# One channel tile as the running sum, and a new order of the first transfers, in a streaming-encoder layer

## The chip, the cores and the metric

The kernel runs on one core of one Trainium2 chip. The metric is the device time of one launch in microseconds (us). The kernel before took 2447.52 us as the median of three runs (2445.77 to 2451.0).

## What is computed

One layer of a streaming encoder, on 512 frames of 2048 channels, all in float32. Two mixers share one normalised input `h`: a gated DeltaNet attention (branch A) and a Conformer convolution module (branch B). The change touches branch B in one place, and the first load of the kernel in another.

```python
h = rmsnorm(x, g_pre[i])
proj = h @ w_in[i]
...
u = jax.nn.glu(glu_in, axis=-1)
u = causal_depthwise_conv(u, w_dw[i]) + b_dw[i]        # 31 taps, 2048 channels
u = jax.nn.silu(layernorm(u, ln_g[i], ln_b[i])) * jax.nn.silu(z_b)
y_b = u @ w_br_b[i]
...
e = p[i] @ w_ple_proj[i]
x = x + rmsnorm(jax.nn.sigmoid(x @ w_ple_gate[i]) * e, g_ple[i])
```

The layernorm needs the sum over all 2048 channels of each frame, so it needs the 16 tiles (128 channels by 512 frames each) of the filtered `u` added up.

## The kernel before, in words

Every float32 product is made of three float32r products: a weight tile is cast to a high part on ScalarE (ACT, L127), the low part is the difference (L128), and each pair of 128 by 128 weights and 128 by 512 activations takes three matmuls (L184, L186, L188: high by high, high by low, low by high). A raw weight load (L122, on SyncE's queue SP, three buffers) holds two pieces of 512 columns; a piece feeds 12 matmuls, and an output tile of the first projection (`gemm_cm`, L171) takes four pieces, 48 matmuls, into one of two PSUM buffers of the pool `gps`. The low part is made on VectorE (DVE) until the heads are done; then `low_part[0]` is set to GpSimd (POOL, L1058).

`load_x` (L226) is the opening. It splits the embedding rows `p` (`embed_in`, L197: two loads `pr`, a cast `ph`, a difference `pl`), loads the first weights of `w_ple_proj` through `prep` (L117), and multiplies the two (`embed`, L209, L216 to L218) while `x` arrives; the transposes that follow (L261) use the identity matrix, the first 128 columns of the tile `cst`, which L97 loads first of all.

Branch B's channels come as pairs of such 48-matmul groups (`glu_pair`, L991). The first group of a pair, for the gate, is taken out of PSUM by ACT (L911); the second by VectorE, which multiplies it with the gate (`evac_glu_a`, L978, the instruction at L981) into a tile `sg` and queues it for the filter. `convs` (L939) filters 14 of the 16 tiles on VectorE: a first scaling by ACT (L933), then 30 instructions of one line, L954, each of which adds a shifted and scaled `u` to the running result `y`. These are held in program order. `near` (L923) copies `u` into PSUM first (L930), if the pool `ups` exists; it does not yet exist for the very first tile, whose `u` is the `sg` tile in SBUF. In the profile the taps of that tile are `uc<-sg,vec,uc`, and those of the others `uc<-up,vec,uc`. `side_convs` (L964) filters two tiles with ACT (L972) and POOL (L973). A finished `y` is stored to DRAM (L961, on SP) for the layernorm to load again.

`filtered` (L915) keeps the channel sum `acc`. The first finished tile is copied into a tile of its own on POOL (L918); each later one is added to it on POOL (L920). `layer_norm` (L1134) multiplies the sum with ones on TensorE (L1143) and goes on from there.

Nothing in the code fixes the order of an engine's queue, save what is pinned: a list scheduler takes the program's instructions in order of priority as its own clock says that they are ready. Each engine and each DMA queue then works through its queue in order; an instruction that waits holds up all behind it.

Of the kernel before, what the change touches and what calls it, by code (L numbers as in the profile page):

```python
# [9 lines left out]
F32 = mybir.dt.float32  # L10
# [5 lines left out]
P = 128  # L16
T = 512
# [64 lines left out]
def _body(ctx, tc, A, out):  # L82
    nc = tc.nc
# [7 lines left out]
    slots = ctx.enter_context(tc.tile_pool(name="slots", bufs=21, side="right"))  # L91
# [2 lines left out]

    cst = const.tile([P, C_COLS], F32, name="cst")
    vec = const.tile([P, V_COLS], F32, name="vec")
    nc.sync.dma_start(cst[:, 0:P], A["consts"][:, 0:P])  # L97
    ident = cst[:, C_ID:C_ID + P]
    half_c = const.tile([P, 8], F32, name="half_c")
    nc.gpsimd.memset(half_c, 0.5)  # L100
# [8 lines left out]
    def vv(col, n=1):  # L109
        return vec[:, col:col + n]  # L110
# [6 lines left out]
    def prep():  # L117
        if not prep_src:
            return
        src = prep_src.popleft()  # L120
        raw = rawp.tile([P, 1024], F32, tag="raw", name="raw", bufs=3)
        nc.sync.dma_start(raw, src)  # L122
        for q in range(2):
            rq = raw[:, q * T:(q + 1) * T]
            w = ring.tile([P, 1024], F32R, tag="w", name="w")
            hi, lo = w[:, 0:T], w[:, T:]
            nc.scalar.copy(hi, rq)  # L127
            low_part[0].tensor_tensor(lo, rq, hi.bitcast(F32), ALU.subtract)  # L128
            hi_lo[id(hi)] = w.rearrange("p (s c) -> p s c", s=2)
            prepped.append((hi, lo))  # L130
# [66 lines left out]
    def embed_in():  # L197
        pT = []
        for k in range(2):
            pr = slots.tile([P, T], F32, tag="s", name="pr")  # L200
            nc.sync.dma_start(pr, A["pT"][k])
            ph = slots.tile([P, T], F32R, tag="s", name="ph")
            nc.scalar.copy(ph, pr)
            pl = slots.tile([P, T], F32R, tag="s", name="pl")
            nc.vector.tensor_tensor(pl, pr, ph.bitcast(F32), ALU.subtract)
            pT.append((ph, pl))
        return pT

    def embed(j, pT, xps):  # L209
        ps = [xps.tile([P, T], F32, tag="xp", name="e_ps") for _ in range(NTT)]  # L210
        for k in range(2):
            wh, wl = prepped.popleft()
            lh, ll = pT[k]
            for tt in range(NTT):
                b = slice(tt * P, (tt + 1) * P)
                mm(ps[tt], lh[:, b], wh, start=k == 0, stop=False)  # L216
                mm(ps[tt], lh[:, b], wl, start=False, stop=False)
                mm(ps[tt], ll[:, b], wh, start=False, stop=k == 1)  # L218
        for tt in range(NTT):
            e = slots.tile([P, T], F32, tag="s", name="e_sb")  # L220
            (nc.vector.tensor_copy if tt % 2 else nc.scalar.copy)(e, ps[tt])
            e_sb[j, tt] = e
# [3 lines left out]
    def load_x():  # L226
        with tc.tile_pool(name="xin", bufs=1) as xin, tc.tile_pool(name="xps", bufs=6, space=PSUM) as xps:
            xs = []
            H = D // 2
            prep_src.extend(A["w_ple_proj"][j] for j in range(4))  # L230
            prep_src.extend(first_src)
            pT = embed_in()
            prep()
            for tt in range(NTT):
                xt = xin.tile([P, D], F32, name=f"x{tt}")
                for hf in range(2):
                    nc.sync.dma_start(xt[:, hf * H:(hf + 1) * H], A["x"][tt * P:(tt + 1) * P, hf * H:(hf + 1) * H])
                if tt == 2:
                    nc.sync.dma_start(vec[:, 0:V_DW], A["vecs"][:, 0:V_DW])
                prep()  # L240
                embed(tt, pT, xps)
                ss = small.tile([P, 2], F32, tag="xss", name="xss")
                junk = xin.tile([P, H], F32, name="xjunk")
                for hf in range(2):
                    nc.scalar.activation(junk, xt[:, hf * H:(hf + 1) * H], AF.Square, accum_out=ss[:, hf:hf + 1])
                ms = small.tile([P, 1], F32, tag="xms", name="xms")
                nc.vector.tensor_tensor(ms, ss[:, 0:1], ss[:, 1:2], ALU.add)
                nc.vector.tensor_scalar(ms, ms, 1.0 / D, EPS, ALU.mult, ALU.add)
                rs = small.tile([P, 1], F32, tag="xrs", name="xrs")
                nc.gpsimd.tensor_tensor(rs, ms, mhalf_c[:, 0:1], ALU.pow)  # L250
                for hf in range(2):
                    nc.vector.tensor_scalar(xt[:, hf * H:(hf + 1) * H], xt[:, hf * H:(hf + 1) * H], rs, None, ALU.mult)
                xs.append(xt)
            nc.sync.dma_start(cst[:, P:], A["consts"][:, P:])
            nc.sync.dma_start(vec[:, V_DW:], A["vecs"][:, V_DW:])
            for (j, tt), e in e_sb.items():
                nc.sync.dma_start(pe_dram[j, tt], e)
            for k in range(NK):
                ps = xps.tile([P, T], F32, tag="xp", name="xp")
                for tt in range(NTT):  # L260
                    nc.tensor.transpose(ps[:, tt * P:(tt + 1) * P], xs[tt][:, k * P:(k + 1) * P], ident)  # L261
                hh = hpool.tile([P, T], F32R, tag="h", name="hh")
                hl = hpool.tile([P, T], F32R, tag="h", name="hl")
                nc.scalar.activation(hh, ps, AF.Copy, scale=vv(V_GPRE + k))
                nc.vector.scalar_tensor_tensor(hl, ps, vv(V_GPRE + k), hh.bitcast(F32), ALU.mult, ALU.subtract)
                hT.append((hh, hl))
# [11 lines left out]

    first_src = [w_in_tile(ZB_TILE0)[0], w_in_tile(ZB_TILE0)[1]]
    load_x()  # L280


# [617 lines left out]
    acc = []  # L900
# [13 lines left out]

    def filtered(i, y):  # L915
        if not acc:
            acc.append(slots.tile([P, T], F32, tag="s", name="acc"))
            nc.gpsimd.tensor_copy(acc[0], y)  # L918
        else:
            nc.gpsimd.tensor_tensor(acc[0], acc[0], y, ALU.add)  # L920
        done.add(i)
# [17 lines left out]
    def convs():  # L939
        ready = last = None  # L940
        while scanning[0] < NH // 2 - 1:
            yield 4
        while len(done) < NK:
            ready = ready or near()
            if not ready:
                if last and len(taken) == NK:
                    filtered(*last)
                    last = None
                yield 1
                continue  # L950
            (i, u, y), ready = ready, None
            w0 = V_DW + i * TAPS
            for s in range(1, TAPS):
                pin(nc.vector.scalar_tensor_tensor(y[:, s:], u[:, 0:T - s], vv(w0 + TAPS - 1 - s), y[:, s:], ALU.mult, ALU.add))  # L954
                if s == 28 and last:
                    filtered(*last)
                    last = None
                if s == 24:
                    ready = near()
                yield pace(s)  # L960
            nc.sync.dma_start(u_dram[i], y)  # L961
            last = i, y

    def side_convs():  # L964
        for _ in range(SIDE):
            while not waiting:
                yield 1
            i, u, y = near(False)
            w0 = V_DW + i * TAPS
            for s in range(1, TAPS):  # L970
                pr = s2.tile([P, T], F32, tag="s2", name="pr")
                nc.scalar.activation(pr[:, s:], u[:, 0:T - s], AF.Copy, scale=vv(w0 + TAPS - 1 - s))  # L972
                pin(nc.gpsimd.tensor_tensor(y[:, s:], y[:, s:], pr[:, s:], ALU.add))  # L973
                yield 18
            nc.sync.dma_start(u_dram[i], y)
            filtered(i, y)
# [643 lines left out]
    for tt in range(NTT):  # L1620
# [9 lines left out]
        for j in range(4):  # L1630
            s = e_t4[tt][j]
# [67 lines left out]
```

## Time and profile before

| | |
|---|---|
| median of three runs | 2447.52 us |
| the profiled execution's own time | 2447.55 us |
| its span, first instruction to last | 2445.8 us |
| TensorE (PE) busy | 2414.0 us, 99% |
| VectorE (DVE) busy | 1792.4 us, 73% |
| ScalarE (ACT) busy | 1208.8 us, 49% |
| GpSimd (POOL) busy | 507.0 us, 21% |
| DMA | 380.21 MB, mean 155 GB/s |

Times in rows of the profile count from the span's start. A row of the timeline is: start, length in us, engine, line, operation, output and inputs by the program's names, shapes, count, and in brackets how long the engine had been idle and what ended that. "SPq" and "ACTq" are the queues of SyncE and ScalarE, which issue DMAs. A matmul of 512 columns is listed at 0.39 us, but the next one starts 0.23 us after it, since they are pipelined. The column PEclk is the clock granted to TensorE as a share of full speed.

### The profile page before, as it was taken

How to read it: one execution, taken by the hardware profiler on the slowest of the kernel's cores; microseconds unless marked ns; L12 is line 12 of the kernel's file. 1: busy time of each engine (PE TensorE's matmuls, PEld its weight loads, DVE VectorE, ACT ScalarE, POOL GpSimd, SP SyncE). 2: the span in 40 equal slices, each digit the busy share in tenths (PEclk: the TensorE clock that was granted, in tenths of full speed). 3: DMA queues.
4: the chain of work that ended last, by engine and by line, in shares of the span. 5: the costliest groups of instructions: out<-in, count | busy, mean ns of one | idle time of the engine just before them, and what ended most of it. 6: DMA issues, size and time to landing. Idle time of an engine off the chain costs nothing.

```text
span 2445.8 us, 33732 instructions
## 1 busy us (share of the span) xinstructions
PE 2414.0 (99%) x11962; PEld 1985.5 (81%) x11962; DVE 1792.4 (73%) x3345; ACT 1208.8 (49%) x2357; POOL 507.0 (21%) x531
## 2 busy tenths in 40 slices
PE   8999999999999999999999998999999999999998
PEld 7888888887888888888888887888887888787886
DVE  7877888777677676867777678998998654667644
ACT  6455544554655656455555544454324533554532
POOL 0001110013213021132300005998740000000000
PEclk9999999999999999999999999999999999999999
DMA  7577776666536263556622222443534333665552
GB/s 270 162 199 199 202 201 208 207 162 204 175 119 185 87 185 93 171 168 178 181 90 90 67 91 79 138 137 104 170 118 166 131 122 99 232 216 173 188 173 77
DMA packets 145289, 380.21 MB, mean 155 GB/s; under 512 B 16352, under 2 KB 24800, under 8 KB 145120
## 3 DMA queue, kind: packets, MB, share of 16 engines
q1 hardware_dynamic: 119008, 319.32, 39.4%
q0 software_dynamic: 23808, 54.54, 10.3%
q10 hardware_dynamic: 2304, 4.20, 0.5%
q8 instruction: 94, 1.54, 0.3%
q14 instruction: 75, 0.61, 0.1%
HBM read 329.75 MB, written 48.23 MB: 155 GB/s over the span
## 4 chain that ended last, share of the span: by engine, by line
PE 89%; DVE 3%; POOL 2%; DMA 2%; issue 2%; ACT 2%; SPq 0%; POOLq 0%; DVEq 0%; ACTq 0%
PE g L186 13%; PE g L188 13%; PE g L184 13%; PE zp L423 6%; PE zp L421 6%; PE zp L422 5%; PE yp L1090 4%; PE yp L1094 4%; PE yp L1092 4%; PE f L1382 2%; PE f L1383 2%; PE f L1384 2%; PE f L1548 2%; PE f L1549 2%; PE f L1550 2%
## 5 line engine op out<-in xcount | busy, mean ns | idle before, releaser
L188 PE MATMUL g<-hh,w 128*128 128x512 f32 x1536 | 610.6, 397 | 4.1 <-POOL w L128 4.1
L186 PE MATMUL g<-hl,w 128*128 128x512 f32 x1536 | 611.3, 398 | 0.0
L184 PE MATMUL g<-hh,w 128*128 128x512 f32 x1536 | 609.5, 397 | 0.0
L127 ACT CAST w<-raw 128x512 fp32r<-128x512 f32 x588 | 357.9, 618 | 446.8 <-PE g L188 172.8
L128 DVE TENSOR_TENSOR w<-raw,w 128x512 fp32r<-128x512 f32 x464 | 321.5, 700 | 169.2 <-ACT w L127 166.6
L188 PEld LDWEIGHTS g<-hh,w 128*128 128x128 f32 x1536 | 289.8, 189 | 61.5 <-POOL w L128 5.4
L186 PEld LDWEIGHTS g<-hl,w 128*128 128x128 f32 x1536 | 289.6, 189 | 55.8 <-issue 1.4
L184 PEld LDWEIGHTS g<-hh,w 128*128 128x128 f32 x1536 | 289.9, 189 | 54.7 <-ACT w L127 0.9
L954 DVE SCALAR_TENSOR_TENSOR uc<-up,vec,uc 128x506 f32<-128x506 f32 (+29 forms) x390 | 284.0, 734 | 11.9
L128 POOL TENSOR_TENSOR w<-raw,w 128x512 fp32r<-128x512 f32 x124 | 161.4, 1314 | 136.7 <-DVE uc L954 74.5
L656 DVE SCALAR_TENSOR_TENSOR cv<-g,vec,cv 128x511 f32<-128x511 f32 x144 | 106.4, 739 | 27.2 <-ACT cv L654 26.6
L1090 PE MATMUL yp<-w,uh 128*128 128x512 f32 x256 | 100.2, 392 | 0.7 <-DVE gt L1102 0.7
L1094 PE MATMUL yp<-w,ul 128*128 128x512 f32 x256 | 100.1, 392 | 0.0
L1090 PE MATMUL yp<-w,oh 128*128 128x512 f32 x256 | 100.0, 393 | 0.0
L1092 PE MATMUL yp<-w,uh 128*128 128x512 f32 x256 | 100.0, 391 | 0.0
L1092 PE MATMUL yp<-w,oh 128*128 128x512 f32 x256 | 99.6, 389 | 0.0
L1094 PE MATMUL yp<-w,ol 128*128 128x512 f32 x256 | 99.1, 389 | 0.0
L842 DVE TENSOR_TENSOR prod<-UT,VT 128x2 f32<-128x2 f32 (+30 forms) x248 | 88.4, 356 | 6.5
L1006 POOL DMA_DIRECT2D wsum<-in_w_out x96 | 76.1, 847 | 71.2 <-DMA wsum<-in_w_out 32.9
L1326 POOL TENSOR_TENSOR rmsm<-totm,mhalf_c 128x2 f32<-128x2 f32 x2 | 2.4, 1198 | 378.3 <-DVE totm L1324 378.3
L973 POOL TENSOR_TENSOR uc<-uc,pr 128x511 f32<-128x511 f32 (+29 forms) x60 | 77.8, 1297 | 3.7 <-ACT pr L972 2.5
L1382 PE MATMUL f<-wsp,oph 128*128 128x512 f32 x192 | 75.6, 394 | 1.7 <-ACT wsp L1363 1.7
(386 smaller groups left out, 4952.5 us busy)
## 6 DMA issues: line engine op xcount, KB each, us to landing
raw<-in_w_in SPq DMA_DIRECT2D x194, 512.0 KB, 3.4
wsum<-in_w_out POOLq DMA_DIRECT2D x96, 256.0 KB, 5.4
raw<-in_w_ple_gate SPq DMA_DIRECT2D x40, 512.0 KB, 3.5
wo_sums<-wsum POOLq DMA_DIRECT2D x64, 256.0 KB, 4.1
raw<-in_w_br_a SPq DMA_DIRECT2D x32, 512.0 KB, 3.4
raw<-in_w_br_b SPq DMA_DIRECT2D x32, 512.0 KB, 3.3
raw<-in_w_ga SPq DMA_DIRECT2D x24, 512.0 KB, 4.7
raw<-in_w_gb SPq DMA_DIRECT2D x24, 512.0 KB, 4.5
```

The costliest lines, as they stand in the source:

```text
L127: nc.scalar.copy(hi, rq)
L128: low_part[0].tensor_tensor(lo, rq, hi.bitcast(F32), ALU.subtract)
L184: mm(ps, wh, rh, start=(k == 0), stop=False)
L186: mm(ps, wh, rl, start=False, stop=False)
L188: mm(ps, wl, rh, start=False, stop=(k == NK - 1))
L421: mm(ps[pr][t], lh, wh, start=q + n == 0, stop=False)
L423: mm(ps[pr][t], lh, wl, start=False, stop=q == 3 and n == 1)
L954: pin(nc.vector.scalar_tensor_tensor(y[:, s:], u[:, 0:T - s], vv(w0 + TAPS - 1 - s), y[:, s:], ALU.mult, ALU.add))
L1090: mm(ps[tt], lh[:, b], wh, start=k == 0, stop=False)
L1092: mm(ps[tt], lh[:, b], wl, start=False, stop=False)
L1094: mm(ps[tt], ll[:, b], wh, start=False, stop=k == NK - 1)
L1382: mm(ps, lh, wh[:, c], start=kk == 0, stop=False)
```

## The change

Three edits. The tile of the first finished channel block becomes the sum itself, in place of a copy of it; the two loads of embedding rows are issued by ScalarE's queue, no longer by SyncE's; and the load of the identity matrix is written behind the first weight load. The identity matrix still comes before the loads of `x`.

```diff
     cst = const.tile([P, C_COLS], F32, name="cst")
     vec = const.tile([P, V_COLS], F32, name="vec")
-    nc.sync.dma_start(cst[:, 0:P], A["consts"][:, 0:P])
     ident = cst[:, C_ID:C_ID + P]
...
             pr = slots.tile([P, T], F32, tag="s", name="pr")
-            nc.sync.dma_start(pr, A["pT"][k])
+            nc.scalar.dma_start(pr, A["pT"][k])
             ph = slots.tile([P, T], F32R, tag="s", name="ph")
...
             pT = embed_in()
             prep()
+            nc.sync.dma_start(cst[:, 0:P], A["consts"][:, 0:P])
             for tt in range(NTT):
...
     def filtered(i, y):
         if not acc:
-            acc.append(slots.tile([P, T], F32, tag="s", name="acc"))
-            nc.gpsimd.tensor_copy(acc[0], y)
+            acc.append(y)
         else:
             nc.gpsimd.tensor_tensor(acc[0], acc[0], y, ALU.add)
```

## The prediction

> **What bounds the kernel now.** I read the page first, then TensorE's waits, then the timeline around the two longest of them.
>
> ```profile
> span 2445.8 us, 33732 instructions
> PE 2414.0 (99%) x11962; PEld 1985.5 (81%) x11962; DVE 1792.4 (73%) x3345; ACT 1208.8 (49%) x2357; POOL 507.0 (21%) x531
> PE e_ps L216 <- ACT w L127: 6.7, 1, 6.7
> PE g L188 <- POOL w L128: 4.1, 2, 3.5
> 1522.00:1527.00 5.00, 5.00 (x14) 3.88 (x13) 4.75 (x8) 1.04 (x3) 5.00 (x5) 0.51 0.68 218
> ```
>
> TensorE is the bound: it is idle for 2445.8 - 2414.0 = 31.8 us in all. Only what moves a TensorE wait can move the time. The opening (6.7 us) is the largest wait, and a wait of 3.5 us for a low part made on POOL is the second; in the stretch after it the granted clock (third figure from the row's end, 0.51) is half. The edits touch just these two places. Both are costed in the profiled execution (2447.55 us, of which the span is 2445.8), which stands 0.03 us from the median of 2447.52. About 0.2%, 4.9 us, is what a measurement of this kernel can tell from no change.
>
> **The wait at 1517, as it is.**
>
> ```profile
> 1509.06 0.39 PE L184 MATMUL g<-hh,w 128*128 128x512 f32 x1
> 1517.45 0.39 PE L186 MATMUL g<-hl,w 128*128 128x512 f32 x1
> 1521.29 0.79 PE L188 MATMUL g<-hh,w 128*128 128x512 f32 x1 [3.45 <-POOL w L128]
> 1525.72 0.63 PE L184 MATMUL g<-hh,w 128*128 128x512 f32 x1
> 1527.20 0.39 PE L186 MATMUL g<-hl,w 128*128 128x512 f32 x1
> 1510.25 1.72 POOL L128 TENSOR_TENSOR w<-raw,w 128x512 fp32r<-128x512 f32 x1
> 1519.40 0.61 POOL L918 COPY acc<-uc 128x512 f32<-128x512 f32 x1 [7.43 <-DVE uc L954]
> 1519.97 1.27 POOL L128 TENSOR_TENSOR w<-raw,w 128x512 fp32r<-128x512 f32 x1
> ```
>
> From 1509.06 to 1517.45 are 37 matmuls, 8.39 / 37 = 0.2268 us each. The next should start at 1517.68; it starts at 1521.29, 3.61 late. The following 14 steps to 1527.20 take 5.91 instead of 14 x 0.227 = 3.18: the half clock costs 2.73 more. Together 6.34 us. The cause is POOL's queue: the copy L918, which waits 7.43 us for the last tap of the first filter, stands ahead of the low part that TensorE needs.
>
> **The sum's copy removed.** POOL goes on at 1511.97 rather than 1519.40, and the low part is there at 1513.7, four microseconds before TensorE asks. If that were all, 6.3 us would be gone. It is not all, because VectorE is in the middle of that first filter.
>
> ```profile
> 1497.40 1.65 DVE L954 SCALAR_TENSOR_TENSOR uc<-sg,vec,uc 128x499 f32<-128x499 f32 x1
> 1510.86 1.64 DVE L954 SCALAR_TENSOR_TENSOR uc<-sg,vec,uc 128x491 f32<-128x491 f32 x1
> 1512.53 0.73 DVE L954 SCALAR_TENSOR_TENSOR uc<-sg,vec,uc 128x490 f32<-128x490 f32 x1
> 1519.26 0.74 DVE L954 SCALAR_TENSOR_TENSOR uc<-up,vec,uc 128x511 f32<-128x511 f32 x1
> 1519.92 0.68 DVE L981 TENSOR_TENSOR sg<-g,sg 128x512 f32<-128x512 f32 x1
> 1495.00:1511.00 16.00, 16.00 (x72) 13.26 (x71) 15.65 (x11) 9.24 (x16) 15.82 (x10) 1.00 0.21 67
> 1521.00:1540.00 19.00, 18.71 (x71) 15.25 (x72) 18.15 (x26) 7.83 (x13) 18.92 (x16) 0.84 0.51 164
> ```
>
> While POOL is busy (15.82 of 16 us from 1495 to 1511) a tap of this filter takes 1.65 us, and a POOL instruction 1.72; from 1497.40 to 1510.86 are eight taps, 13.46 / 8 = 1.68 from start to start. When POOL falls silent the same tap takes 0.73. The later filters, whose `u` lies in PSUM (`up`), do not suffer: from 1521 to 1540 POOL is busy for 18.92 of 19 us and taps still take 0.74. So the wait of POOL is also a free road for VectorE: the nine taps from 1512.53 to 1519.26 (6.73 / 9 = 0.75 from start to start) ran fast only because the copy held POOL. Does POOL have nine instructions' worth of ready work to put in their place?
>
> ```profile
> 1522.43 2.53 POOL L128 TENSOR_TENSOR w<-raw,w 128x512 fp32r<-128x512 f32 x2
> 1528.61 1.32 POOL L1069 TENSOR_TENSOR ol<-oa,oh 128x512 fp32r<-128x512 f32 x1
> 1529.86 2.58 POOL L128 TENSOR_TENSOR w<-raw,w 128x512 fp32r<-128x512 f32 x2
> 1501.79 2.55 ACT L972 ACTIVATE pr<-sg,vec 128x507 f32<-128x507 f32 x4
> 1515.29 1.14 ACT L1067 CAST oh<-oa 128x512 fp32r<-128x512 f32 x2
> 1517.47 0.62 ACT L127 CAST w<-raw 128x512 fp32r<-128x512 f32 x1 [1.04 <-issue]
> 1525.96 0.60 ACT L911 ACTIVATE sg<-g 128x512 f32<-128x512 f32 x1 [7.88 <-PE g L188]
> ```
>
> Behind the copy POOL runs, from 1519.97 to about 1531, without a gap: a low part, a side tap (L973), two low parts, a side tap, a head's low part (L1069), a side tap, another L1069, a low part. That is nine (11.2 us at about 1.25 each), and their inputs come from ACT: side products by 1504.3, casts of the heads by 1516.4, the last weight cast by 1518.1, all before POOL would reach them at one per 1.68 us. So all nine taps stay slow: the first ends its turn not at 1513.3 but at 1514.2, and the ninth at 1512.53 + 9 x 1.68 = 1527.65. Behind them in VectorE's queue stand one tap of the next filter and then L981, which now end 1519.92 + 0.68 - 1519.26 = 1.34 after the ninth tap; that gives 1528.99.
>
> Who waits for L981? It empties one of two PSUM buffers. The group that fills it began its successor at 1509.06 in the other buffer; that successor is 48 matmuls long and so would end at 1509.06 + 48 x 0.2268 = 1519.94 without a stall. In the trace its end is 1525.72, and ACT's L911 empties it at 1525.96. The next group must have L981's buffer. Today it is free at 1520.60, five microseconds early. After the change TensorE would stand from 1519.94 to 1529.04 (0.05 for the hand-over, as from POOL's 1521.24 to 1521.29): 9.10 us, and then run at half clock again.
>
> The price of that clock phase: 2.73 us at 1521, and in the opening
>
> ```profile
> 6.68 0.80 PE L216 MATMUL e_ps<-w,ph 128*128 128x512 f32 x1 [6.68 <-ACT w L127]
> 11.87 0.39 PE L216 MATMUL e_ps<-w,ph 128*128 128x512 f32 x1
> 13.36 0.50 PE L218 MATMUL e_ps<-w,pl 128*128 128x512 f32 x1 [0.64 <-DVE pl L205]
> ```
>
> 12 steps take 5.19 instead of 2.72, a loss of 2.47. I take 2.6. [...] So the place costs 9.1 + 2.6 = 11.7 after, 6.3 before: **+5.4 us**. Bounds: 2.2 to 3.2 for the clock and one tap (1.0) either way for the overlap give +4 to +7.
>
> What else moves there: the copy's own 0.61 us on POOL lies under TensorE's work. SP's store of the tile (L961) waits for the ninth tap too, and raw loads stand behind it; but the three raw buffers hold the pieces of the whole next group, which is on the wrong side of the stall. The next add L920 on POOL must wait for the second filter:
>
> ```profile
> 1543.30 0.59 ACT L930 COPY up<-sg 128x512 f32<-128x512 f32 x1 [2.53 <-DVE uc L954]
> 1545.08 1.30 POOL L920 TENSOR_TENSOR acc<-acc,uc 128x512 f32<-128x512 f32 x1
> 1546.34 1.30 POOL L128 TENSOR_TENSOR w<-raw,w 128x512 fp32r<-128x512 f32 x1
> 1551.24 0.39 PE L188 MATMUL g<-hh,w 128*128 128x512 f32 x1
>   PE g L188: 9.4, 7
> ```
>
> That filter ends with L930's release at 1543.3, and 8.4 later after the change, so the add comes at 1551.7, 6.6 later, with a low part behind it that TensorE uses 3.6 us after it is made (1547.64 to 1551.24). TensorE itself is 5.4 later: 1.2 of the 3.6 is eaten, nothing waits. VectorE then catches up: from 1520 to 1760 it sat idle before L981 seven times, 9.4 us (last row), waiting for TensorE, which is more than the 3 us that it is further behind.
>
> **The opening.**
>
> ```profile
> 0.74 0.38 SPq L97 DMA_DIRECT2D cst<-in_consts  x1
> 1.17 0.42 SPq L201 DMA_DIRECT2D pr<-in_pT  x1
> 1.64 0.42 SPq L122 DMA_DIRECT2D raw<-in_w_ple_proj  x1
> 6.01 1.14 ACT L127 CAST w<-raw 128x512 fp32r<-128x512 f32 x2 [1.49 <-DMA raw<-in_w_ple_proj]
> 12.62 0.68 DVE L205 TENSOR_TENSOR pl<-pr,ph 128x512 fp32r<-128x512 f32 x1
> ```
>
> TensorE starts 0.67 after that cast, which starts when `raw` lands. The issue of `raw` moves from 1.64 to 0.74, 0.9 us. ACT takes two issues (0.4 each) before data that it must wait for anyway. The same bytes are in flight, so the gain at 6.68 lies between 0 and the 0.9, or a little over since the small identity packets no longer go first. The 0.64 us before 13.36 is a wait for the second embedding row's low part, which VectorE makes at 12.62 behind work on `x`; if the row's earlier load brings it forward, that wait goes as well, and if not, it swallows what was won at 6.68. Between 0 and -2 I take **-1.2 us**. The identity matrix, one issue later, is first needed by the transposes behind all this, so it costs nothing; were it late, its 0.38 us issue is the price.
>
> Sum: 2447.55 + 5.4 - 1.2 = **2451.7 us**, 0.17% more: no change that a measurement would show, from a gain and a loss.
>
> **Rivals.** *The stall simply goes.* If the scheduler puts L981 ahead of the slow taps, or POOL's and VectorE's instructions overlap better than ten rows at 1.68 say, the buffer is free in time: 2447.55 - 6.3 - 1.2 = 2440.0. For it: the low part does come in time, and the order of VectorE's queue is the scheduler's, which no row shows for the changed program. Against it: L981 stands behind those taps today.
>
> *The engines exclude each other wholly.* Then a pair costs the two lengths alone, 1.27 + 0.73 = 2.00 instead of 1.68; nine pairs take 18.0, not 15.1, and L981 and TensorE come 2.9 us later: 2454.6, slower. It decides from a pair spacing of about 1.76 up, where nine pairs add the 0.7 us that are missing to 4.9. Ten rows in a row at 1.68 speak against it. [...]
>
> *The change does not free POOL.* If another instruction that waits for that filter takes the copy's place in POOL's queue, the stall stays: 2447.55 - 1.2 = 2446.3. The first add is the only candidate, and it needs the second filter as well, at 1545.08, so this is unlikely.
>
> **How the numbers follow.** My forecast's case has 0.58; of it 0.11 lies above 4.9 us (no gain in the opening gives 2447.55 + 5.4 = 2452.9). The vanishing stall has 0.25, the full lock 0.09, the stall that stays 0.08. Faster: 0.25. Same: 0.47 + 0.08 = 0.55. Slower: 0.11 + 0.09 = 0.20. The range must reach into the first rival to hold 8 in 10: 2439.0 to 2454.0; the forecast's own is 2449.5 to 2454.
>
> **What would show it.** Right: no L918; POOL without a gap after about 1510; nine more taps at 1.65; L981 about 8 us later; a TensorE wait of some 9 us on DVE L981 at the start of a group, then half clock; a first matmul near 5.8. Wrong: no TensorE wait at that place (first rival), a pair spacing near 2.0 (second), or POOL still waiting for DVE L954 (third).

## The result, and the profile after

The change made the kernel slower: 2455.32 us (median of seven runs, 2453.04 to 2458.22) against 2446.80 (seven runs of the kernel before beside it, 2445.04 to 2451.0). The ratio is 1.0033, with a 95% interval of 1.0022 to 1.0045: 8 us, with 5 to 11 us possible. The forecast was 2451.7 with a range up to 2454.0. The profiled execution took 2456.29 us. In the kernel after, most lines have moved up by one (the filter's taps are L953, the evacuation on VectorE is L980).

The page and TensorE's waits of the kernel after (in the waits: microseconds in total, how often, the longest):

```profile
span 2454.2 us, 33730 instructions
PE 2415.4 (98%) x11962; PEld 1986.8 (81%) x11962; DVE 1799.3 (73%) x3345; ACT 1209.2 (49%) x2357; POOL 510.6 (21%) x530
PE g L183 <- DVE sg L980: 9.8, 1, 9.8
PE e_ps L215 <- ACT w L126: 6.3, 1, 6.3
PE e_ps L215 <- ACT ph L202: 1.1, 1, 1.1
```

TensorE's longest wait is a new one. The wait for POOL at 1517 is gone from the list; in its place TensorE stands 9.8 us for the instruction by which VectorE empties a PSUM buffer. The timeline of the kernel after at that place:

```profile
1495.16 34.37 DVE L953 SCALAR_TENSOR_TENSOR uc<-sg,vec,uc 128x502 f32<-128x502 f32 x21
1515.76 3.40 POOL L127 TENSOR_TENSOR w<-raw,w 128x512 fp32r<-128x512 f32 x2
1519.13 1.70 POOL L972 TENSOR_TENSOR uc<-uc,pr 128x505 f32<-128x505 f32 x1
1520.79 1.69 POOL L1068 TENSOR_TENSOR ol<-oa,oh 128x512 fp32r<-128x512 f32 x1
1522.44 1.67 POOL L972 TENSOR_TENSOR uc<-uc,pr 128x504 f32<-128x504 f32 x1
1524.07 3.32 POOL L127 TENSOR_TENSOR w<-raw,w 128x512 fp32r<-128x512 f32 x2
1527.35 1.66 POOL L972 TENSOR_TENSOR uc<-uc,pr 128x503 f32<-128x503 f32 x1
1529.45 0.74 DVE L953 SCALAR_TENSOR_TENSOR uc<-up,vec,uc 128x511 f32<-128x511 f32 x1
1530.11 0.67 DVE L980 TENSOR_TENSOR sg<-g,sg 128x512 f32<-128x512 f32 x1
1520.70 0.39 PE L187 MATMUL g<-hh,w 128*128 128x512 f32 x1
1530.93 0.77 PE L183 MATMUL g<-hh,w 128*128 128x512 f32 x1 [9.84 <-DVE sg L980]
1537.04 0.40 PE L187 MATMUL g<-hh,w 128*128 128x512 f32 x1
```

The same 21 taps in the kernel before:

```profile
1494.17 25.17 DVE L954 SCALAR_TENSOR_TENSOR uc<-sg,vec,uc 128x502 f32<-128x502 f32 x21
```

Read the POOL rows first: each starts where the one before ends, so POOL no longer waits for the filter. The price stands in the first row: the 21 taps with both inputs in SBUF take 34.37 us, 9.20 more than before. From POOL's 1515.76 to 1527.35 are seven instructions, 11.59 / 7 = 1.66 us each, where the prediction had 1.68. Behind the last of the 21 taps come one tap of the next filter and then L980, which starts at 1530.11 and ends at 1530.78. TensorE, whose next matmul was due at 1520.70 + 0.23 = 1520.93, goes on at 1530.93. The 14 steps from there to 1537.04 take 6.11 us instead of 3.18, at half clock (granted 0.50). So the place costs 10.00 + 2.93 = 12.9 us, against 6.34 before: 6.6 more.

Set each matmul beside the same one of the profile before: the first of the kernel comes 0.4 us earlier, the one at 23.6 us 0.3 later, those near 1000 us at the same time, those from 1100 to 1480 1.1 later, those behind the stall 7.6 later, the last 8.4 later.

The opening of the kernel after:

```profile
0.74 0.38 SPq L121 DMA_DIRECT2D raw<-in_w_ple_proj  x1
0.74 0.40 ACTq L200 DMA_DIRECT2D pr<-in_pT  x1
5.08 0.62 ACT L202 CAST ph<-pr 128x512 fp32r<-128x512 f32 x1 [2.62 <-DMA pr<-in_pT]
5.08 0.35 ACTq L200 DMA_DIRECT2D pr<-in_pT  x1
5.60 1.13 ACT L126 CAST w<-raw 128x512 fp32r<-128x512 f32 x2
6.26 0.79 PE L215 MATMUL e_ps<-w,ph 128*128 128x512 f32 x1 [6.26 <-ACT w L126]
12.28 0.62 ACT L202 CAST ph<-pr 128x512 fp32r<-128x512 f32 x1 [2.83 <-DMA pr<-in_pT]
12.95 0.50 PE L215 MATMUL e_ps<-w,ph 128*128 128x512 f32 x1 [1.14 <-ACT ph L202]
```

The two first loads now leave together at 0.74, and the embedding rows land at 5.08 (before: 3.90). The weights' cast waits for no load any more: it stands behind the rows' cast on ScalarE, so it starts at 5.60 and TensorE at 6.26 rather than 6.68. The second load of rows is issued at 5.08, when ScalarE reaches it behind that first cast; before, SyncE issued it at 3.06. It lands late, its cast comes at 12.28, and TensorE waits 1.14 us for it.

### The profile page after: what moved, and what is told of

The parts are those of the page before. It is cut to its first block, busy times and chain, and to the rows that moved or that the text cites. A ratio compares the mean times of both kernels' runs of the same rounds, so it can differ in the third digit from the quotient of the medians.

```text
span 2454.2 us, 33730 instructions
## 1 busy us (share of the span) xinstructions
PE 2415.4 (98%) x11962; PEld 1986.8 (81%) x11962; DVE 1799.3 (73%) x3345; ACT 1209.2 (49%) x2357; POOL 510.6 (21%) x530
## 3 DMA queue, kind: packets, MB, share of 16 engines
q0 software_dynamic: 23808, 54.54, 10.2%
## 4 chain that ended last, share of the span: by engine, by line
PE 88%; DVE 5%; DMA 2%; POOL 2%; ACT 2%; issue 1%; SPq 0%; POOLq 0%; DVEq 0%; ACTq 0%
PE g L185 13%; PE g L187 13%; PE g L183 13%; PE zp L423 6%; PE zp L422 6%; PE zp L421 6%; PE yp L1089 4%; PE yp L1091 4%; PE yp L1093 4%; PE f L1381 2%; PE f L1382 2%; PE f L1383 2%; PE f L1549 2%; PE f L1548 2%; PE f L1547 2%; DVE uc L953 2%
## 5 line engine op out<-in xcount | busy, mean ns | idle before, releaser
L183 PEld LDWEIGHTS g<-hh,w 128*128 128x128 f32 x1536 | 290.3, 189 | 65.8 <-issue 10.2
L953 DVE SCALAR_TENSOR_TENSOR uc<-up,vec,uc 128x506 f32<-128x506 f32 (+29 forms) x390 | 283.9, 733 | 11.9
```

Of the source, the lines that this page charges most:

```text
L183: mm(ps, wh, rh, start=(k == 0), stop=False)
```

## The experiments

The theory is that of the prediction, made into a chain: POOL works on; it collides with the first filter's taps, because that filter alone reads its input from SBUF (before the change, beside a busy POOL: 1.65 us a tap, against 0.74 with the input in PSUM); the filter ends late; whatever waits for its end or stands behind it on VectorE is late, a PSUM buffer first of all. Against it stand two others: that the edits of the opening cost the time, or that the first tile, now held as the sum, does. In the list, times are medians, ratios are against runs of the kernel before on the same chip, with 95% intervals. The kernel before took 2445.58 us beside the first four kernels, 2446.01 beside the next four, 2446.03 beside the last four.

| run | median us | ratio | interval |
|---|---|---|---|
| the sum alone | 2451.79 | 1.0026 | 1.0015 to 1.0037 |
| the opening alone | 2447.61 | 1.0007 | 0.9999 to 1.0016 |
| the change, with POOL's wait, without the copy | 2446.48 | 1.0005 | 0.9996 to 1.0014 |
| the change, more PSUM buffers | 2453.16 | 1.0035 | 1.0022 to 1.0047 |
| the sum, first filter later | 2442.58 | 0.9987 | 0.9978 to 0.9996 |
| the sum, first filter's input to PSUM | 2439.69 | 0.9976 | 0.9966 to 0.9985 |
| the copy kept, first filter's input to PSUM | 2439.38 | 0.9972 | 0.9962 to 0.9983 |
| the sum, input to PSUM, opening in another order | 2438.77 | 0.9971 | 0.9961 to 0.9982 |
| rows on ScalarE's queue alone | 2447.47 | 1.0008 | 0.9999 to 1.0017 |
| identity matrix later alone | 2445.79 | 1.0000 | 0.9991 to 1.0009 |
| opening in another order alone | 2445.63 | 1.0002 | 0.9993 to 1.0011 |
| the change, input to PSUM | 2440.42 | 0.9979 | 0.9970 to 0.9988 |

**The sum alone, on the kernel before.**

```diff
-            acc.append(slots.tile([P, T], F32, tag="s", name="acc"))
-            nc.gpsimd.tensor_copy(acc[0], y)
+            acc.append(y)
```

> The kernel before with the edit of the sum alone; the opening is left as it was. Collision theory (with no copy to wait for, POOL works on beside the first filter, whose taps have both inputs in SBUF and so take 1.65 rather than 0.73 us; the evacuation that frees TensorE's PSUM buffer comes late): the whole loss is here, 2453 to 2456 us, with a TensorE wait of 9 to 10 us for the DVE instruction on sg near 1520, 21 taps in 34 us and some 13 us at half clock after it. Opening theory (the moved loads cost the time, the sum does not): 2446 to 2448 us, no change. The two stalls of about half a microsecond in the heads stage (1077 and 1089), which the changed kernel has and the kernel before has not: if they come from the opening, they are absent here and the time is nearer 2454; if from the sum, they cannot be, since they stand ahead of it.

Slower by 6.2 us (3.7 to 9.1 by the interval). Its timeline and its waits have the chain of the kernel after:

```profile
1493.14 33.23 DVE L953 SCALAR_TENSOR_TENSOR uc<-sg,vec,uc 128x502 f32<-128x502 f32 x21
PE g L184 <- DVE sg L980: 8.7, 1, 8.7
```

Most of the loss is the sum's. It is less than the 2453 to 2456 us expected: the wait is 8.7 us, not 9 to 10, and the half clock behind it lasted 10.2 us, not 13. Its matmuls lie 1.0 us ahead of those of before at 1510 and 4.0 behind at 1626: 5.0 us for the place in this execution.

**The opening alone: the changed kernel with the copy put back.**

```diff
-            acc.append(y)
+            acc.append(slots.tile([P, T], F32, tag="s", name="acc"))
+            nc.gpsimd.tensor_copy(acc[0], y)
```

> The changed kernel with the copy into a tile of its own put back: the opening edits alone. Collision theory: 2446 to 2449 us, within 0.2% of the kernel before; POOL waits 7 us for the last tap again, TensorE waits 3.5 us for a low part made on POOL near 1517, and no wait of 9 us. The opening itself gives its first wait back (6.3 against 6.7 us, then 1.1 against 0.6 us at the second half). Opening theory: 2453 to 2456 us. If the two half-microsecond stalls near 1077 and 1089 are seen here as well, they come from the opening edits and cost about 1 us: 2448.

Slower by 2.0 us, with -0.2 to +3.9 by the interval: no loss is shown, but a gain of 1.2 is outside it. The matmuls of its profile lie 0.3 us behind those of before at 23.6 us, and the last ones level with them. The waits of before are back (3.5 us for POOL's low part), that of 9 us is not there. The opening theory falls for the large part.

**POOL's wait without the copy.**

```diff
             acc.append(y)
+            seen = small.tile([P, 1], F32, tag="seen", name="seen")
+            nc.gpsimd.tensor_copy(seen, y[:, T - 1:T])
```

> The changed kernel, in which POOL copies one column of the first finished channel into a tile of its own (nothing reads it), so that POOL waits for the last tap as before, but the copy of 512 columns is left out and the finished tile still serves as the sum. Collision theory: the wait, not the copy, was what mattered; POOL idles about 7 us, 21 taps take about 25 us again, TensorE's wait is 3 to 3.5 us for the low part and not 9.8 us for VectorE, and the time is 2446 to 2449 us. Theory that the tile kept as the sum costs the time (its place in the pool of tiles is held longer, the first addition waits for it): 2455 us as in the changed kernel, with the wait of 9 to 10 us still there or another in its place.

```profile
1518.69 0.19 POOL L919 COPY seen<-uc 128x1 f32<-128x1 f32 x1 [7.44 <-DVE uc L955]
1493.45 25.18 DVE L955 SCALAR_TENSOR_TENSOR uc<-sg,vec,uc 128x502 f32<-128x502 f32 x21
PE g L187 <- POOL w L127: 3.7, 2, 3.0
```

0.9 us over the kernel before and, by the two ratios (1.0005 and 1.0033), 7 us under the changed one, although it has the same sum and the same opening. An instruction of 0.19 us that does nothing but wait 7.44 us makes the kernel faster by that much: while POOL stands, VectorE has the road for itself and ends its 21 taps in 25.18 us, not 34.37. The tile that serves as the sum costs nothing by itself.

**More PSUM buffers, in the changed kernel.**

```diff
-            ps = gps.tile([P, T], F32, tag="g", name="g")
+            ps = yps.tile([P, T], F32, tag="y", name="g") if early else gps.tile([P, T], F32, tag="g", name="g")
...
-        gemm_cm(w_in_tile(GLU_TILE0 + i), hT, evac_glu_a(i))
+        gemm_cm(w_in_tile(GLU_TILE0 + i), hT, evac_glu_a(i), 5 <= i < 10)
```

> The changed kernel with five groups of gated matmuls (numbers 5 to 9, those that stand around the first filter) put into another set of PSUM buffers, so that TensorE does not wait for the evacuation at the end of the filter. Collision theory in two steps, collision first and then the buffer: the taps stay at 1.65 us (POOL still works beside them), but the wait of 9.8 us for the DVE instruction and the half clock behind it go, and the time falls by 12 to 16 us to 2440 to 2444 us. If the buffer is not the link (TensorE would wait for something else that VectorE owes it just as late, or the other set is itself not free), the time stays at 2452 to 2456 us and the wait only changes its name.

The miss: 12 to 16 us were expected of it and it brought nothing that shows. The wait for L980 is gone, and two others stand in its place. The timeline (SyncE's queue, ScalarE, TensorE):

```profile
1527.03 0.33 SPq L960 DMA_DIRECT2D u_dram<-uc  x1
1527.45 0.38 SPq L121 DMA_DIRECT2D raw<-in_w_in  x1
1532.02 0.62 ACT L126 CAST w<-raw 128x512 fp32r<-128x512 f32 x1 [9.37 <-DMA raw<-in_w_in]
1532.69 0.62 PE L183 MATMUL g<-hh,w 128*128 128x512 f32 x1 [2.19 <-ACT w L126]
1550.95 0.59 ACT L929 COPY up<-sg 128x512 f32<-128x512 f32 x1 [12.59 <-DVE uc L953]
1552.14 0.51 PE L183 MATMUL g<-hh,w 128*128 128x512 f32 x1 [3.10 <-ACT w L126]
```

The store of the finished channel (L960) waits on SyncE's queue for the last tap, and the next weights are issued only behind it, at 1527.45; they land at 1532.02 and TensorE waits 2.19 us. Later ScalarE stands 12.59 us before the copy L929, which waits for VectorE, with weight casts behind it, and TensorE waits 3.10 us more. The PSUM buffer was the first of three links to the late filter; with it gone, the next two are met. So the middle of the chain, not its last link, has to be mended.

**The first filter later, with its input in PSUM.** The sum as in the change, without the copy, and the opening as before.

```diff
-        while scanning[0] < NH // 2 - 1:
+        while scanning[0] < NH // 2 - 1 or not ups:
             yield 4
```

> The kernel before with the edit of the sum, and the first filter does not begin until the PSUM pool for the filters' input exists, so that its input, like that of all the others, is copied into PSUM; POOL works on beside it as in the changed kernel. Collision theory: the taps take 0.74 us although POOL is busy all the time, the first filter ends no later than before (30 taps by 0.67 to 0.77 us from some 1497: 1517 to 1520), neither the wait of 3.6 us for POOL nor that of 9 us for VectorE is left, and the time is 2438 to 2443 us. If POOL's work slows VectorE whatever the place of its input, the taps stay at 1.65 us, the filter ends near 1545 and the time is 2455 us or more. If holding the tile as the sum were a cost of its own, 2450 us or more with taps at 0.74 us.

3.4 us under the kernel before, and no wait from 1500 to 1780 is left. Its taps (`uc<-up,vec,uc`) go at 14.70 us for 19, 0.77 each. It is 2.9 us slower than the next kernel. Its matmuls, set beside those of before, lose 4.0 us between 1760 and 2035, those of the next kernel nothing; TensorE waits there for VectorE's `gt` (1.10 us) and for a low part made there (1.09 us). Why was not pursued.

**The first filter's input moved to PSUM as soon as the pool exists.**

```diff
             for s in range(1, TAPS):
+                if ups and not held:
+                    held = True
+                    up = ups.tile([P, T], F32, tag="u", name="up")
+                    nc.scalar.copy(up, u)
+                    u = up
```

> The kernel before with the edit of the sum; the first filter begins as early as before, and as soon as the PSUM pool exists, its input is copied there by ScalarE (one copy of 0.6 us) and the taps left read it from PSUM. Collision theory: the 20 taps left take 0.67 to 0.77 us instead of 1.65 us, the first filter ends 5 us earlier than before (about 1514), no wait at 1517 to 1530 is left, and the time falls by the whole 6.3 us of the stall and its half clock: 2438 to 2441 us. If VectorE's lateness was not what TensorE waited for, 2450 to 2455 us as with the edit of the sum alone.

The timeline, and one row of the stretches (us, busy time and count of TensorE, its weight loads, VectorE, ScalarE, POOL; then the granted clock); the last row is the same stretch of the kernel after:

```profile
1492.79 14.52 DVE L959 SCALAR_TENSOR_TENSOR uc<-up,vec,uc 128x502 f32<-128x502 f32 x19
1507.98 0.69 DVE L986 TENSOR_TENSOR sg<-g,sg 128x512 f32<-128x512 f32 x1 [0.67 <-PE g L188]
1504.82 1.30 POOL L978 TENSOR_TENSOR uc<-uc,pr 128x507 f32<-128x507 f32 x1
1511.00:1527.00 16.00, 16.00 (x73) 13.23 (x72) 15.26 (x21) 8.53 (x16) 13.53 (x12) 1.00 0.44 147
```

```profile
1511.00:1527.00 16.00, 10.09 (x45) 8.03 (x43) 15.65 (x11) 5.37 (x9) 16.00 (x10) 0.89 0.05 20
```

TensorE is busy without a gap (73 matmuls instead of 45), at full clock (1.00 granted, against 0.89); VectorE does 21 instructions in the time of 11, and POOL's own fall from 1.7 to 1.3 us. VectorE even waits for TensorE before the evacuation, 0.67 us. The time is 6.3 us under the kernel before, as much as the whole stall of 1517 cost, and 12.1 us under the same kernel with the input left in SBUF, by medians. One copy of 0.6 us on ScalarE does it. The collision is the cause.

**The same, but with the copy kept.**

```diff
             acc.append(slots.tile([P, T], F32, tag="s", name="acc"))
             nc.gpsimd.tensor_copy(acc[0], y)
```

> The kernel before, with its copy of the first channel on POOL, and only the input of the first filter moved into PSUM as in the run before this one. Collision theory: the copy waits for a filter that now ends near 1513, while TensorE needs POOL's low part only at 1517.7, so the wait behind the copy becomes short enough to be hidden: 2438 to 2442 us, within 0.1% of the same kernel without the copy. The edit of the sum is then worth nothing, neither gain nor loss. If the copy cost TensorE something by itself, the stall of 3.5 us stays and the time is 2445 to 2448 us.

```profile
1510.87 0.61 POOL L918 COPY acc<-uc 128x512 f32<-128x512 f32 x1
```

The copy stands in the same place of POOL's queue and waits for nothing, because the filter has ended. 2439.38 against 2439.69: without the collision, the edit of the sum is worth nothing that can be measured, either way.

**The opening in another order.**

```diff
+        prs = [slots.tile([P, T], F32, tag="s", name="pr") for _ in range(2)]
         for k in range(2):
-            pr = slots.tile([P, T], F32, tag="s", name="pr")
-            nc.scalar.dma_start(pr, A["pT"][k])
+            nc.scalar.dma_start(prs[k], A["pT"][k])
+        for k in range(2):
+            pr = prs[k]
             ph = slots.tile([P, T], F32R, tag="s", name="ph")
```

> The edit of the sum and the first filter's input in PSUM, with the changed opening in another order: both loads of embedding rows are issued on ScalarE's queue ahead of the first cast, so that the second does not stand behind a cast that waits for the first. If the opening of the change lost its gain by that order alone, the first matmul starts at 5.8 to 6.4 us, the second half's wait of 1.1 us falls to 0.6 us or less, and the time is 0.5 to 1.5 us under the same kernel with the old opening, which a comparison can hardly tell; the profile can. If the loads are bound by something else (they share the DMA engines with the first weights and x), the second half still waits 1 us or more and the time is the same within 0.5 us.

> The kernel before with the whole opening of the change, but both row loads issued on ScalarE's queue ahead of the first cast; the sum is left as it was, with its copy and its stall. Queue-order theory: the second half's wait of 1.1 us is gone and the kernel is 0.5 to 1.5 us under the opening of the change alone (2447.61 us against 2445.58): 2445 to 2447 us. If the opening edits cost time by something else (loads of x that come later, say): 2447 to 2449 us again.

**The two edits of the opening, one at a time** (`nc.sync` to `nc.scalar` for the rows; the identity's load behind `prep()`).

> The kernel before with one of the opening's two edits: the embedding rows are loaded on ScalarE's queue, the identity matrix still comes first of all. Queue-order theory (the second row load is issued only when ScalarE reaches it, behind the cast that waits for the first): the second load is issued near 4 us or later rather than at 3.06, lands after 10.7 us, and TensorE waits about 1 us for the second half's high part; what the earlier weights win at the start is lost there: 2445 to 2449 us. If moving the rows brings a gain of its own, as the forecast's -1.2 us had it: 2444.5 us, and no wait for the high part near 13 us.

> The kernel before with the other edit of the opening: the identity matrix is loaded behind the first weights, the rows stay on SyncE's queue. The first weights are issued at 1.2 rather than 1.64 us, so the first matmul may come up to 0.45 us earlier; the second row load is issued about as before and no wait for ScalarE's high part appears. Queue-order theory: 2445 to 2447 us, 0.4 us better at best, and better than the kernel with the rows moved, if the two can be told apart at all. If the whole opening's loss of some 2 us (0.07% measured, within its uncertainty) is real and sits in the identity matrix, 2448 us.

By their times the last three of these four kernels can't be told from the kernel before, nor can the first, which has the sum's edit and the input in PSUM, from the kernel with these two and the old opening (2438.77 against 2439.69). The profiles can tell what happens. First the rows on ScalarE's queue alone, then the identity later, then both loads of rows ahead of the casts:

```profile
5.01 0.35 ACTq L201 DMA_DIRECT2D pr<-in_pT  x1
5.68 0.80 PE L216 MATMUL e_ps<-w,ph 128*128 128x512 f32 x1 [5.68 <-ACT w L127]
13.03 0.50 PE L216 MATMUL e_ps<-w,ph 128*128 128x512 f32 x1 [1.85 <-ACT ph L203]
```

```profile
5.73 0.80 PE L215 MATMUL e_ps<-w,ph 128*128 128x512 f32 x1 [5.73 <-ACT w L126]
13.48 0.74 PE L217 MATMUL e_ps<-w,pl 128*128 128x512 f32 x2 [0.29 <-DVE pl L204]
```

```profile
0.73 0.89 ACTq L200 DMA_DIRECT2D pr<-in_pT  x2
6.12 0.61 ACT L204 CAST ph<-pr 128x512 fp32r<-128x512 f32 x1
6.26 0.80 PE L217 MATMUL e_ps<-w,ph 128*128 128x512 f32 x1 [6.26 <-ACT w L126]
```

Each edit alone brings the first matmul forward to 5.7 (five profiles with the old opening: 6.2 to 7.2). Both together do not: in five profiles with the change's own opening it stands at 6.3 to 6.6. In the seven profiles in which the rows and the first weights leave together at 0.74, ScalarE can cast the first rows only at 5.1 to 5.4; in the seven others, where they leave 0.4 us or more apart, at 3.5 to 4.0. Why they land later together was not tested. With the rows on ScalarE's queue the second load is issued at 5.01, behind the first cast, and 1.85 us are lost for it at 13.03. With both loads issued ahead of the casts, the second cast ends at 6.73, five microseconds before the second half's first matmul (11.93), and no wait for the second half is left. At the matmul that stands at 23.6 us in the profile before, the three lie 2.1 behind, 0.35 ahead and 0.42 ahead; the five profiles with the change's own opening lie 0.25 to 0.42 behind, the other four with the old one from 0.57 ahead to 0.58 behind. So the late second issue comes from the queue order; that it costs 1 to 2 us of time is not shown.

**The whole change with the input in PSUM.**

> The whole change, opening included, and the first filter's input moved into PSUM when the pool exists. Collision theory: the 9.8 us wait and its half clock are gone and so is the old 3.5 us wait; 2438 to 2442 us, 13 to 16 us under the changed kernel. Beside the same kernel with the old opening (0.9976 of the kernel before) it shows the opening's worth once more: about equal, or up to 2 us above it if the opening edits cost time.

Against the changed kernel the ratios 0.9979 and 1.0033 differ by 0.0054, 13.2 us; the same kernel with the old opening is 0.7 us lower, within the uncertainty. Five of the twelve kernels beat both that before and that after, and all five have the first filter's input in PSUM; four of them, with the sum's edit or without, with the old opening or either new one, lie within 1.7 us of each other.

## Why the prediction was wrong

**The step that failed is the opening, -1.2 us.** Its sentence was that "ACT takes two issues (0.4 each) before data that it must wait for anyway". One of the two issues does stand there. The other stands behind a cast that waits for the first load, so it left at 5.08 instead of 3.06; the second load came later and not earlier, and the second half waited 1.14 us where it had waited 0.64. The start also won less than the 0.9 us that the weights' issue moved: the rows landed at 5.08 instead of 3.90, and their cast is ahead of the weights' on ScalarE, so 0.42 was left. Single profiles scatter here: with the old opening the five have their first matmul at 6.2 to 7.2 and wait 0 to 1.5 us in the second half, with the change's five it is 6.3 to 6.6 and 0.5 to 1.5. At 23.6 us the change's five lie inside the range of the old ones, with nothing won. Alone, the opening measured +2.0 us (-0.2 to +3.9), where the bounds had been 0 and -2; a gain of 1.2 lies outside the interval, a loss is not shown. The order could have been seen in the program, where each pass of the loop issues a load, casts it, and only then issues the next.

**The place at 1517: right mechanism, nearly the right size.** Forecast +5.4 (bounds +4 to +7). The kernel with this edit alone measured +6.2 (3.7 to 9.1), its profile +5.0, that of the whole change +6.6. The nine taps are right: 10 of the 21 take more than 1.5 us before, 19 in the sum alone and 20 in the kernel after. With nine more, in the sum alone, TensorE stood 8.7 us. The tenth of the kernel after, which the bounds had allowed for, stands at the front of the row, where POOL was already at work, and the wait is 10.0 and not 9.1. The half clock cost 2.93, not 2.6.

**Why the sum came out too low.** The last matmul of the profile after lies 8.4 us behind that of before, where 4.2 were forecast. Of these 8.4 us, 0.3 are lost by 23.6 us, 0.7 from there to 1510, 6.6 at the place and 0.8 behind it. So the gain in the opening that did not come makes 1.5 of the missing 4.2, the place 1.2, and 1.5 lie elsewhere. With no gain in the opening the forecast's own text gave 2452.9; with the medians of the two parts measured alone, 6.2 + 2.0, it would have been 2447.55 + 8.2 = 2455.8, but the 2.0 is not clear of nothing. The range had no room for this: its top, 2454.0, even lies below the sum of the forecast's own bounds, 2447.55 + 7 + 0 = 2454.55.

**What held.** No copy; POOL without a gap; taps at 1.64 us (median of 21); the end of L980 at 1530.78 (forecast 1528.99; this profile was 1.0 us behind at 1510, and the tenth tap takes 0.9 more); a TensorE wait of more than 9 us on it, then half clock. The first matmul, expected near 5.8, came at 6.26. The wait for the next add did not become a new one: TensorE waits 0.63 us at the layernorm's sum in both profiles.

**The rivals.** That the stall simply goes is what happens once the collision is gone (2439.69, forecast 2440.0 with an opening's gain that isn't there), but not by this change. That the engines exclude each other wholly, 2.00 us for a pair, falls: 1.66 us in the kernel after, and in the sum alone eleven POOL instructions from 1507.56 to 1525.82, again 18.26 / 11 = 1.66. With POOL at work, a tap of this filter takes 34.37 / 21 = 1.64 us with its input in SBUF, and 14.52 / 19 = 0.76 with its input in PSUM. In the slow pairs neither engine stood for the other's whole length: both engines lose, POOL 0.4 us and VectorE 0.9 us, and the pair takes 0.3 us less than the sum of their lengths.

**What stays open.** In the profile after, 1.1 us were lost near 1077 and 1089 in the heads' stage, ahead of any edit but the opening, and 0.8 in pieces behind 1626. Waits of 0.35 to 0.50 us at 1087 to 1089 are also in five of the other profiles, one of them with the old opening, and the stretch up to 1480 ends anywhere from 2.6 us ahead of the profile before to 1.1 behind it. They may be the scatter of single executions; that was not tested. Open as well are why the first loads land later when they leave together, and why the kernel with the first filter later loses 4.0 us behind 1760.

## What to carry to other kernels

An engine that stands waiting can be the reason why its neighbour is quick (here 25.18 us for 21 taps while POOL waited 7.44 us, 34.37 us while it worked): before a wait is taken away, ask what the waiting engine will do instead, and with whom that collides. Where a whole stretch ends late, look for what made it long, since a buffer more here only passed the lateness to the next queues that waited for the same end (a store in front of weight loads, 2.19 us of TensorE, then a copy in front of casts, 3.10 us). The DMA moved to a compute engine's queue was issued when that engine reached it (here at 5.08 us, behind a cast, instead of 3.06): put such a load in the program ahead of whatever waits for data.

## What the runs showed of the hardware

The half clock came in whole pieces of 3.41 us. The stretches of the kernel after, cut where the granted clock changes, and three pieces of the kernel with POOL's wait and no copy:

```profile
1489.25:1492.67 3.42, 3.42 (x10) 2.63 (x11) 1.35 (x6) 0.00 (x0) 1.01 (x1) 0.50 0.20 77
1492.67:1523.39 30.72, 28.42 (x128) 23.18 (x126) 29.54 (x24) 16.06 (x27) 28.51 (x18) 1.00 0.16 52
1523.39:1537.04 13.65, 6.11 (x14) 4.79 (x15) 13.26 (x15) 1.29 (x4) 5.62 (x4) 0.50 0.46 166
```

```profile
1516.55:1519.96 3.41, 0.56 (x3) 0.14 (x1) 3.34 (x6) 0.62 (x1) 1.27 (x2) 1.00 0.13 52
1519.96:1523.38 3.42, 3.23 (x8) 2.55 (x9) 3.28 (x5) 0.00 (x0) 3.42 (x4) 0.50 0.66 235
1523.38:1526.79 3.41, 3.41 (x17) 2.82 (x16) 3.25 (x5) 2.57 (x5) 3.41 (x4) 1.00 0.50 174
```

The lengths in the first fence are one, nine and four such pieces: 3.42 us, 30.72 / 9 = 3.41 and 13.65 / 4 = 3.41.

In the kernel after, the piece in which TensorE resumes (1530.22 to 1533.63) is busy from 1530.93, 79% of it, and the next piece is still at half clock; in the other kernel the piece at half clock is 94% busy, and the next is at full clock. The other profiles bear this out. The fourteen of them, cut into such pieces from the first recorded change of the clock to 2425 us, have 24 pieces at half clock: the eight in which TensorE is busy for 0 to 81% are followed by another at half clock, the sixteen with 91 to 100% by full clock. Of the pieces at full clock, the sixteen with 0 to 46% are followed by half clock, and all others, with 51% or more, by full clock.

So stalls of nearly the same length differed by about a microsecond in what followed them, as they fell differently in these pieces. The stalls of 3.04, 3.68 and 3.71 us (POOL's wait without the copy, rows on ScalarE's queue, identity later) were followed by one piece at half clock, and 1.60, 1.74 and 1.77 us were lost in it. Those of 3.45, 3.47 and 3.48 us (the kernel before, the opening alone, the opening in another order alone) were followed by two pieces and lost 2.74, 3.03 and 2.86. That the kernel after lost 2.93, and not 1.6 to 1.8 like the first three, agrees with where its stall ended: 0.71 us into a piece, which was then busy for 79% and was followed by another at half clock. The forecast took its 2.6 from losses of 2.73 and 2.47; nothing in its rows told which case the new stall would be, so that it came near is in part luck.
